# Strassen's seven products for the first feed-forward matrix, its result kept in DRAM

## The chip, the cores and the metric

One core of a Trainium2 chip runs the whole program. The metric is the device time of one execution in microseconds (us), as the median of several runs; one more execution, taken by the hardware profiler, gives the trace. Engines are named as in the profile: PE is TensorE's matrix multiplication and PEld its weight loading, DVE is VectorE, ACT is ScalarE, POOL is GpSimd, SP is SyncE, which here only issues DMAs.

## What is computed

One layer of a decoder for 1024 prompt tokens and 8 sample tokens, in fp32. Width D is 1024, the hidden width of the feed-forward part 2816, in 22 blocks of 128.

```
mod = silu(c) @ w_ada + b_ada            -> shift1, scale1, gate1, shift2, scale2, gate2
h   = x * (1 + scale1) + shift1
[q,k,v | rq,rk,rv,rg | ga,gb] = h @ w_in
A   = dilated window attention(q,k,v) @ w_att_out
B   = (silu(rg) * groupnorm(retention(rq,rk,rv))) @ w_ret_out
x   = LN1(alpha * x + gate1 * ((sigmoid(ga) * A + sigmoid(gb) * B) @ w_o))
f_gate, f_up = split((x * (1 + scale2) + shift2) @ w_ffn_in)
x   = LN2(alpha * x + gate2 * ((silu(f_gate) * f_up) @ w_ffn_out))
```

The outputs are both x, the prompt's caches and state, and the sample caches moved on by one row (rolled).

## The kernel before

Activations lie transposed in SBUF, features on the 128 partitions and tokens along the columns. An fp32 product is made of three products of rounded parts: `mm3` (L186 to L193) does hi x hi, hi x lo and lo x hi for each block k of 128 input features, and accumulates in PSUM. Weights come in by `wload`/`wcols` (L172 to L184): an SP-queue DMA of 512 KB into a raw buffer, a ScalarE cast to hi (L154), a subtraction for lo (L155) on VectorE, or on POOL for `w_o`. Raw, hi and lo have three buffers each; other tiles live in equal slots that are handed out and taken back in program order. PSUM banks are `dbank` (three), `abank` and `bbank` (two each), `obank` (one). A list scheduler orders each engine's instructions by modelled readiness, and each engine and queue then works in that order.

`dense` (L195 to L201) runs one weight block over the token chunks and calls the evacuation of each. The modulation for the later gates (`ada_rest`, L227 to L238) is 8 groups of 512 columns in four sub-steps of two k each; `dense` calls one sub-step after each chunk (`between`), in the gate stages at L844 and L855. The retention projection at L874 adds into the mix, stored as hi and lo (L866 to L872).

The `w_o` stage (L922 to L970) goes over the token chunks of TLAST, widths 392, 384 and 256 in this order, the first with the sample tokens: eight output blocks with `w_o` loaded anew for each chunk, then for every 128 tokens transposes back to token rows, layer norm, a store of the normalised rows to the DRAM tensor `xr`, transposes again, modulation and the split into `h2` hi and lo.

The feed-forward loop (L1029 to L1056) goes over portions of 6, 6, 6 and 4 hidden blocks. For each block f, gate and up weights are loaded, and for each token chunk come 24 matmuls for the gate, 24 for up, SiLU on ScalarE (L1041), the product on VectorE (L1044) and the split of `ff`. After a portion the second matrix goes over the portion's k, and `add_out` (L976) adds the gated result into `acc` in SBUF. The last portion's second matrix is resident (`load_resident`, L1016) and is run chunk by chunk (L1087) with the transposes (L1109), the residual, and `finish` (L1062), the second layer norm and store. `residual` (L1003) prepares alpha x from `xr` into `xo` during the loop.

The cache rolls are DMAs from DRAM to DRAM, on POOL's queue, one for each weight load while `rolling` is on (`roll`, L162): 78 entries, 24 of them empty spacers, 16 copies of 2 MB.

## Time and profile before

| | us |
|---|---|
| time, median of 3 runs | 1929.05 (1927.33 to 1930.64) |
| profiled execution, its own time | 1928.9 |
| its span in the trace | 1927.1 |
| PE busy | 1879.8 (98%) |
| DVE, ACT, POOL busy | 793.9, 551.3, 233.1 |
| mean granted clock of TensorE, share of full | 0.994 |

The trace's times count from the start of the span. A row of a timeline has start, duration, engine, line, operation, output and inputs, and in brackets the idle time before it and what ended that. A matmul's duration reaches into the next one, so the pitch is read from start to start.

### The profile page before, as it was taken

What the parts mean: (1) busy time and instruction counts of PE and PEld (TensorE: products, weight loads), DVE (VectorE), ACT (ScalarE), POOL (GpSimd) and SP (SyncE); (2) the same over time, 40 slices, a digit from 0 to 9 for tenths busy, and PEclk for the clock granted to TensorE, in tenths of its full rate; (3) what the DMA queues carried; (4) which work ended last, traced back from release to release, by engine and by line L of the source; (5) the groups of instructions that cost most, each with busy time, mean ns of one, the idle gap of its engine ahead of it and who ended that gap; (6) DMA issues with size and microseconds to landing.
All of it is one profiled execution on the core that took longest, in us unless ns stands there. A gap on an engine that the chain in (4) does not pass through costs nothing.

```text
span 1927.1 us, 29754 instructions
## 1 busy us (share of the span) xinstructions
PE 1879.8 (98%) x12406; PEld 1770.6 (92%) x12406; DVE 793.9 (41%) x1824; ACT 551.3 (29%) x1118; POOL 233.1 (12%) x313
## 2 busy tenths in 40 slices
PE   7999999999999999999999999999999999999996
PEld 5879889889899988889999999999999999999996
DVE  4733636676434431221453673221133332332337
ACT  3252332443434341121322553122222111211212
POOL 2000010320100000000003551000010000000015
PEclk9999999999999999999999999999999999999998
DMA  9312131681322343351123562223253643334332
GB/s 275 101 37 95 35 104 33 162 277 52 102 57 67 94 137 107 115 164 53 55 66 101 164 201 85 85 66 126 77 186 131 208 139 124 132 132 142 110 111 88
DMA packets 211016, 221.41 MB, mean 115 GB/s; under 512 B 7765, under 2 KB 186301, under 8 KB 210114
## 3 DMA queue, kind: packets, MB, share of 16 engines
q1 hardware_dynamic: 192338, 119.60, 21.7%
q0 software_dynamic: 18416, 99.82, 14.7%
q8 instruction: 97, 1.59, 0.3%
q14 instruction: 37, 0.30, 0.1%
q10 hardware_dynamic: 128, 0.10, 0.0%
HBM read 195.98 MB, written 67.54 MB: 137 GB/s over the span
## 4 chain that ended last, share of the span: by engine, by line
PE 88%; DVE 4%; DMA 3%; ACT 2%; issue 2%; SPq 1%; POOL 1%; DVEq 0%; POOLq 0%; ACTq 0%
PE ps_d L191 24%; PE ps_d L192 23%; PE ps_d L193 23%; PE ps_d L359 2%; PE ps_d L357 2%; PE ps_d L358 2%; DMA w_raw<-w_in 2%; PE ps_a L224 2%; PE ps_a L473 2%; PE ps_b L491 1%; PE ps_o L500 1%; DMA vb<-dv 1%; PE ps_o L745 1%; PE ps_a L747 1%; DVE h_lo L155 1%
## 5 line engine op out<-in xcount | busy, mean ns | idle before, releaser
L191 PE MATMUL ps_d<-h_hi,w_hi 128*128 128x384 f32 (+3 forms) x2064 | 664.4, 322 | 0.6 <-ACT tm L1041 0.6
L192 PE MATMUL ps_d<-h_lo,w_hi 128*128 128x384 f32 (+3 forms) x2064 | 662.0, 321 | 0.0
L193 PE MATMUL ps_d<-h_hi,w_lo 128*128 128x384 f32 (+3 forms) x2064 | 661.0, 320 | 0.0
L191 PEld LDWEIGHTS ps_d<-h_hi,w_hi 128*128 128x128 f32 x2064 | 388.2, 188 | 22.9 <-issue 17.3
L193 PEld LDWEIGHTS ps_d<-h_hi,w_lo 128*128 128x128 f32 x2064 | 388.2, 188 | 1.7 <-issue 1.2
L192 PEld LDWEIGHTS ps_d<-h_lo,w_hi 128*128 128x128 f32 x2064 | 388.0, 188 | 0.8 <-issue 0.4
L154 ACT CAST w_hi<-w_raw 128x1024 fp32r<-128x1024 f32 (+2 forms) x164 | 161.7, 987 | 479.1 <-PE ps_d L192 410.9
L155 DVE TENSOR_TENSOR w_lo<-w_raw,w_hi 128x1024 fp32r<-128x1024 f32 (+2 forms) x140 | 158.4, 1131 | 324.9 <-ACT w_hi L154 324.3
L1044 DVE TENSOR_TENSOR tm<-tm,ps_d 128x392 f32<-128x392 f32 (+2 forms) x66 | 33.8, 513 | 272.9 <-PE ps_d L193 271.4
L192 PE MATMUL ps_d<-ff_lo,w_hi 128*128 128x384 f32 (+1 forms) x432 | 138.2, 320 | 0.0
L191 PE MATMUL ps_d<-ff_hi,w_hi 128*128 128x384 f32 (+1 forms) x432 | 138.1, 320 | 0.0
L193 PE MATMUL ps_d<-ff_hi,w_lo 128*128 128x384 f32 (+1 forms) x432 | 138.1, 320 | 0.0
L359 PE MATMUL ps_d<-w_lo,h_hi 128*128 128x256 f32 x448 | 127.0, 284 | 0.7 <-DVE w_lo L155 0.7
L357 PE MATMUL ps_d<-w_hi,h_hi 128*128 128x256 f32 x448 | 127.4, 285 | 0.0
L358 PE MATMUL ps_d<-w_hi,h_lo 128*128 128x256 f32 x448 | 126.2, 282 | 0.0
L168 POOL COPY tick<-tk 1x1 f32<-1x1 f32 x54 | 11.2, 207 | 704.1 <-DVE tk L167 704.1
L357 PEld LDWEIGHTS ps_d<-w_hi,h_hi 128*128 128x128 f32 x448 | 84.3, 188 | 3.6 <-issue 3.1
L359 PEld LDWEIGHTS ps_d<-w_lo,h_hi 128*128 128x128 f32 x448 | 84.3, 188 | 2.7 <-issue 1.9
L154 ACT CAST ff_hi<-tm 128x392 fp32r<-128x392 f32 (+2 forms) x66 | 31.5, 477 | 188.4 <-DVE tm L1044 188.4
L358 PEld LDWEIGHTS ps_d<-w_hi,h_lo 128*128 128x128 f32 x448 | 84.4, 188 | 0.9 <-issue 0.7
L191 PEld LDWEIGHTS ps_d<-ff_hi,w_hi 128*128 128x128 f32 x432 | 81.3, 188 | 0.0
L192 PEld LDWEIGHTS ps_d<-ff_lo,w_hi 128*128 128x128 f32 x432 | 81.2, 188 | 0.0
(325 smaller groups left out, 2725.4 us busy)
## 6 DMA issues: line engine op xcount, KB each, us to landing
w_raw<-w_in SPq DMA_DIRECT2D x56, 512.0 KB, 4.1
w_raw<-w_ffn_in SPq DMA_DIRECT2D x44, 512.0 KB, 3.9
ada_raw<-w_ada SPq DMA_DIRECT2D x32, 512.0 KB, 4.6
sample_k<-cache_k POOLq DMA_DIRECT2D x8, 2047.0 KB, 10.2
sample_v<-cache_v POOLq DMA_DIRECT2D x8, 2047.0 KB, 10.0
w_raw<-w_o SPq DMA_DIRECT2D x24, 512.0 KB, 4.6
w_raw<-w_ffn_out SPq DMA_DIRECT2D x24, 384.0 KB, 4.4
ada_raw<-w_ada SPq DMA_DIRECT2D x32, 256.0 KB, 5.4
```

What stands on the lines that cost most here:

```text
L154: nc.scalar.copy(hi, raw)
L155: eng.tensor_sub(lo, raw, hi.bitcast(F32))
L191: nc.tensor.matmul(ps, whi[:, k0 + k, :], xhi[:, t0:t0 + n], start=f, stop=False)
L192: nc.tensor.matmul(ps, whi[:, k0 + k, :], xlo[:, t0:t0 + n], start=False, stop=False)
L193: nc.tensor.matmul(ps, wlo[:, k0 + k, :], xhi[:, t0:t0 + n], start=False, stop=l)
L224: nc.tensor.matmul(ps[32 * g:32 * g + 32], cs[:, k0 + k, :], w[:, k], start=k0 + k < 4, stop=k0 + k >= 4)
L357: nc.tensor.matmul(ps[:, j, :], xh, whi, start=k == 0, stop=False)
L358: nc.tensor.matmul(ps[:, j, :], xl, whi, start=False, stop=False)
L359: nc.tensor.matmul(ps[:, j, :], xh, wlo, start=False, stop=k == 7)
L473: nc.tensor.matmul(sb[hh][:, p, :nk], qT[p][r, 128 * bi:128 * bi + 128], kT[p][r, k0:k0 + nk], start=True, stop=True)
L491: nc.tensor.transpose(pb[:, j, :], pm[h][:, 128 * b:128 * b + 128], ident[:])
L1044: nc.vector.tensor_mul(tm[:, :n], tm[:, :n], pu)
```

## The change

The first feed-forward matrix is computed by Strassen's scheme (seven block products in place of eight). A 2 x 2 block product is taken over two halves of the input features, gate and up columns, and two token blocks of each 512-token half. For each half seven combinations X of the normalised input are made once (`combine`: four subtractions and seven splits for each 256-token chunk). For each hidden block, `pair_load` loads the gate and up weights (512 KB each) and makes the sums on POOL, `pair_split` splits them into hi and lo, and `pair_half` runs seven products of 12 matmuls with 260 (half 1) or 256 columns (half 0), adds the products up, and does SiLU and the product with up. The result of each block goes to the DRAM tensor `ffd`. The jobs run half 1 alone for the first three hidden blocks, both halves for the next 19, and half 0 for the first three at the end.

The second matrix then runs for half 1 and for half 0: the 22 blocks are read back and split (`xk`), the sum over all 22 k stays in PSUM, `w_ffn_out` is loaded for each half. `acc`, `xo` and the resident weights are gone; the residual is prepared on POOL when y is loaded. `w_o` and the retention projection go over chunks of 256, 256, 256 and 264 columns, `w_o` from the last chunk to the first. The later modulation is 16 steps of 256 columns over all k, one after each `dense` of the stages at L844 and L845.

```diff
-PORTIONS = (6, 6, 6, 4)
-TLAST = ((640, 392), (0, 384), (384, 256))
+QCH = ((0, 256), (256, 256), (512, 256), (768, 264))
+HALF = (256, 260)
+LEAD = 3
...
     def ada_rest():
-        for cg in range(4, 12):
-            ps = abank((128, 512))
-            for k0 in range(0, 8, 2):
-                raw = slots.alloc((128, 2, 512), name="ada_raw")
...
+        for cg in range(8, 24):
+            ps = abank((128, 256))
+            raws = [slots.alloc((128, 4, 256), name="ada_raw") for _ in range(2)]
...
-        dense(wcols(a["w_att_out"], 128 * f, nk=2), oa, mul)
+        dense(wcols(a["w_att_out"], 128 * f, nk=2), oa, mul, between=ada)
...
-        dense(wcols(w_in, C_GB + 128 * f), hT, sig, between=ada if f < 4 else None)
+        dense(wcols(w_in, C_GB + 128 * f), hT, sig)
...
-        dense(wcols(a["w_ret_out"], 128 * f), gs, evac)
+        dense(wcols(a["w_ret_out"], 128 * f), gs, evac, chunks=QCH)
...
+    def combine(X, c, x11, x21, x12, x22):
+        def put(p, v):
+            split(v, X[p][0][:, :, c], X[p][1][:, :, c])
+        put(1, x11)
+        put(2, x21)
+        put(3, x22)
+        nc.vector.tensor_sub(x11, x12, x11)
+        nc.vector.tensor_sub(x12, x22, x12)
+        nc.vector.tensor_sub(x22, x22, x11)
+        nc.vector.tensor_sub(x21, x21, x22)
+        put(6, x22)
+        put(5, x11)
+        put(7, x12)
+        put(4, x21)
...
+    def pair_load(i):
+        g, u, s_ = [stream.tile([128, 8, 128], F32, tag="raw", name="w_raw") for _ in range(3)]
+        for t, c0 in ((g, 128 * i), (u, D_FF + 128 * i)):
+            dma_w.dma_start(t[:], w_fi[:, c0:c0 + 128].rearrange("(k p) c -> p k c", p=128))
+        nc.gpsimd.tensor_add(s_[:, 4:8, :], u[:, 0:4, :], u[:, 4:8, :])
+        nc.gpsimd.tensor_sub(s_[:, 0:4, :], s_[:, 4:8, :], g[:, 0:4, :])
+        nc.gpsimd.tensor_sub(u[:, 0:4, :], g[:, 0:4, :], u[:, 0:4, :])
...
+    def pair_split(i, j):
...
+        if j < 3:
+            split((g, s_, u)[j][:], hi[:], lo[:])
+        else:
+            nc.gpsimd.tensor_sub(g[:, 4:8, :], g[:, 4:8, :], s_[:, 0:4, :])
+            split(g[:, 4:8, :], hi[:, 0:4, :], lo[:, 0:4, :])
+        if rolling[0]:
+            roll(hi)
...
+    def pair_half(i, half, after):
+        n, x = HALF[half], X[half]
+        t = slots.alloc((128, 4, 260), name="c4")
+        s1, u2, u3, c22 = [t[:, j, :n] for j in range(4)]
+        pa = obank((128, n))
+        product(pa, i, 0, 0, x[1], n, True)
+        nc.scalar.copy(s1, pa)
+        pg = dbank((128, n))
+        product(pg, i, 0, 1, x[2], n, True)
+        nc.vector.tensor_add(s1, s1, pg)
+        after(0)
+        product(pa, i, 1, 0, x[6], n, False)
+        nc.scalar.copy(u2, pa)
+        pd = dbank((128, n))
+        product(pd, i, 1, 1, x[5], n, True)
+        after(1)
+        product(pa, i, 2, 0, x[7], n, False)
+        nc.scalar.copy(u3, pa)
+        nc.vector.tensor_add(c22, u3, pd)
+        pf = dbank((128, n))
+        product(pf, i, 2, 1, x[4], n, True)
+        after(2)
+        nc.vector.tensor_add(u3, u3, pf)
+        product(pd, i, 3, 0, x[3], n, False)
+        after(3)
+        nc.vector.tensor_add(u2, u2, pd)
+        ff = slots.alloc((128, 2, 260), name="ff")
+        for j, (g, u) in enumerate(((s1, u3), (u2, c22))):
+            nc.scalar.activation(g, g, AF.Silu)
+            nc.vector.tensor_mul(ff[:, j, :n], g, u)
...
+        dma_o.dma_start(ffd[i, half].rearrange("p (a b) -> p a b", a=2)[:, :, :n], ff[:, :, :n])
...
+    for ci in (3, 2, 1, 0):
+        t0, n = QCH[ci]
...
+        if ci % 2 == 0:
+            X[ci // 2] = new_x()
+            combine_chunk(ci + 1)
+            combine_chunk(ci)
+
+    jobs = [(i, (1,)) for i in range(LEAD)] + [(i, (1, 0)) for i in range(LEAD, FFC)] + [(i, (0,)) for i in range(LEAD)]
+    rolling[0] = True
+    for q, (i, halves) in enumerate(jobs):
+        nxt = jobs[q + 1][0] if q + 1 < len(jobs) else None
...
+        if nxt is not None:
+            pair_load(nxt)
+            pair_split(nxt, 0)
+        for half in halves:
+            def after(j):
+                if half != halves[-1]:
+                    return
+                pair_drop(i, j)
+                if nxt is not None and j < 3:
+                    pair_split(nxt, j + 1)
+            pair_half(i, half, after)
...
+    for half in (1, 0):
+        n = HALF[half]
+        order = list(range(LEAD, FFC)) + list(range(LEAD))
+        xk = {}
+        for k in order:
+            raw = slots.alloc((128, 2, 260), name="ffr")
+            nc.sync.dma_start(raw[:, :, :n], ffd[k, half].rearrange("p (a b) -> p a b", a=2)[:, :, :n])
+            xk[k] = slots.alloc((128, 2, 2, 260), F32R, name="xk")
+            split(raw[:, :, :n], xk[k][:, 0, :, :n], xk[k][:, 1, :, :n])
...
+            for op, t in zip((OP.mult, OP.add), ln1):
+                nc.gpsimd.tensor_tensor(y[:rows], y[:rows], t[:rows], op=op)
...
+        for f in range(8):
+            pss = [dbank((128, n)) for _ in range(2)]
...
+            for k0, nk in ((0, 8), (8, 8), (16, 6)):
+                whi, wlo = wcols(w_fo, 128 * f, nk=nk, k0=k0)
+                for j, ps in enumerate(pss):
+                    for kk in range(nk):
+                        k = k0 + kk
+                        nc.tensor.matmul(ps, whi[:, kk, :], xk[k][:, 0, j, :n], start=k == 0, stop=False)
+                        nc.tensor.matmul(ps, whi[:, kk, :], xk[k][:, 1, j, :n], start=False, stop=False)
+                        nc.tensor.matmul(ps, wlo[:, kk, :], xk[k][:, 0, j, :n], start=False, stop=k == FFC - 1)
```

## Rows read from the trace of the kernel before

**Rows 1.** The page, part 1: busy us, share of the span, instructions.
```profile
PE 1879.8 (98%) x12406; PEld 1770.6 (92%) x12406; DVE 793.9 (41%) x1824; ACT 551.3 (29%) x1118; POOL 233.1 (12%) x313
```
**Rows 2.** Windows, feed-forward loop: window, length, PE, PEld, DVE, ACT, POOL, clock, DMA, GB/s.
```profile
1165.00:1864.00 699.00, 698.40 (x4440) 698.08 (x4439) 200.55 (x354) 138.81 (x227) 41.22 (x105) 1.00 0.36 123
```
**Rows 3.** Timeline of PE: first matmuls of runs with 256, 264, 384 columns.
```profile
1238.35 0.28 PE L191 MATMUL ps_d<-h_hi,w_hi 128*128 128x256 f32 x1
...
1244.02 0.34 PE L191 MATMUL ps_d<-h_hi,w_hi 128*128 128x392 f32 x1
...
1304.16 0.29 PE L191 MATMUL ps_d<-ff_hi,w_hi 128*128 128x264 f32 x1
...
1306.35 0.34 PE L191 MATMUL ps_d<-ff_hi,w_hi 128*128 128x384 f32 x1
...
1312.66 0.29 PE L191 MATMUL ps_d<-ff_hi,w_hi 128*128 128x264 f32 x1
```
**Rows 4.** Timeline of PE: first matmuls of w_o, FFN block, second matrix, next, last stage.
```profile
1037.66 0.45 PE L191 MATMUL ps_d<-m_hi,w_hi 128*128 128x392 f32 x1
...
1176.06 0.34 PE L191 MATMUL ps_d<-h_hi,w_hi 128*128 128x392 f32 x1
...
1289.33 0.34 PE L191 MATMUL ps_d<-ff_hi,w_hi 128*128 128x384 f32 x1
...
1357.39 0.34 PE L191 MATMUL ps_d<-h_hi,w_hi 128*128 128x392 f32 x1
...
1856.05 0.34 PE L191 MATMUL ps_d<-ff_hi,wr_hi 128*128 128x392 f32 x1
...
1915.98 0.45 PE L1109 MATMUL ps_a<-ident,acc 128*128 128x128 f32 x1 [2.09 <-DVE acc L984]
```
**Rows 5.** The chain that ended last: modulation of both shapes, and eight transposes.
```profile
33.54 1.00 PE ps_b L224 x16
...
706.86 0.98 PE ps_a L224 x4
...
1156.18 0.89 PE ps_b L952 x8
```
**Rows 6.** Groups by form: count, busy us, mean ns, idle before and its releasers.
```profile
L154 ACT CAST w_hi<-w_raw 128x1024 fp32r<-128x1024 f32 x132 | 138.4, 1050 | 357.1 <-PE ps_d L192 288.9 <-POOL w_lo L155 27.5 <-PE ps_d L358 26.4
L155 DVE TENSOR_TENSOR w_lo<-w_raw,w_hi 128x1024 fp32r<-128x1024 f32 x108 | 132.0, 1222 | 229.3 <-ACT w_hi L154 228.8
L155 POOL TENSOR_TENSOR w_lo<-w_raw,w_hi 128x1024 fp32r<-128x1024 f32 x24 | 57.9, 2414 | 47.6 <-ACT w_hi L154 47.5
...
L155 DVE TENSOR_TENSOR w_lo<-w_raw,w_hi 128x768 fp32r<-128x768 f32 x24 | 23.0, 958 | 44.1 <-ACT w_hi L154 43.9
```
**Rows 7.** Timeline of POOL, then of DVE, at the end of a w_o chunk.
```profile
1136.69 0.58 POOL L947 DMA_DIRECT2D xr<-x  x1 [2.87 <-DVE x L911]
1137.29 4.75 POOL L155 TENSOR_TENSOR w_lo<-w_raw,w_hi 128x1024 fp32r<-128x1024 f32 x2
1142.30 2.57 POOL L155 TENSOR_TENSOR w_lo<-w_raw,w_hi 128x1024 fp32r<-128x1024 f32 x1 [0.26 <-ACT w_hi L154]
...
1138.42 7.41 DVE L155 TENSOR_TENSOR h_lo<-tm,h_hi 128x128 fp32r<-128x128 f32 x8
```
**Rows 8.** Landings: weights, 1165 to 1860; then a cache copy issued at 1584.2.
```profile
DMA to landing us min/median/max: 3.3/3.9/9.3
...
DMA to landing us min/median/max: 10.0/10.0/10.0
```
**Rows 9.** The chain, then a window as in rows 2, around a late weight load.
```profile
367.10 27.07 DMA w_raw<-w_in
...
394.00:402.00 8.00, 5.90 (x24) 5.41 (x24) 5.35 (x9) 2.73 (x6) 0.10 (x1) 0.60 1.05 358
```
**Rows 10.** Timeline of DVE, tail: first and last of 14 operations for two blocks.
```profile
1916.89 0.75 DVE L1110 TENSOR_TENSOR y<-y,ps_a 128x256 f32<-128x256 f32 x2 [0.67 <-PE ps_a L1109]
...
1921.03 2.73 DVE L1081 SCALAR_TENSOR_TENSOR y<-y,bnr,ln_b 128x512 f32<-128x512 f32 x4
```

More of the change, by code (lines that the diff above doesn't have):

```diff
@@ L199, in dense @@
             evac(t0, n, ps)
-            if between:
-                next(between, None)
+        if between:
+            next(between, None)
     w_ada, w_in = a["w_ada"], a["w_in"]
@@ L912, in layer_norm @@
                                 op0=OP.subtract, op1=OP.mult)
[L914 to L916 removed]
     xr = dram.tile([T, D], F32, name="xr")
[L919 removed]
+    ffd = dram.tile([FFC, 2, 128, 520], F32, name="ffd")
+    w_fi, w_fo = a["w_ffn_in"], a["w_ffn_out"]
     rolling[0] = False
[L921 removed]
@@ new lines, in combine, with new_x @@
+    def combine(X, c, x11, x21, x12, x22):
[12 more added lines that the diff above has]
+        put(4, x21)
+    def new_x():
+        return {p: [slots.alloc((128, 4, 260), F32R, name=f"X{p}") for _ in range(2)] for p in range(1, 8)}
@@ new lines, in free_x, with combine_chunk @@
+    def free_x(X):
+        for t in X.values():
+            slots.free(*t)
+    h2s = late.tile([128, 8, NB], F32, name="h2s")
+    H2 = {}
+    X = [None, None]
+    def combine_chunk(ci):
+        p = slice(128 * (ci % 2), 128 * (ci % 2) + 128)
+        e, d = H2.pop(2 * ci), H2.pop(2 * ci + 1)
+        combine(X[ci // 2], p, e[:, 0:4, :], e[:, 4:8, :], d[:, 0:4, :], d[:, 4:8, :])
+        slots.free(e, d)
+        if ci == 3:
+            combine(X[1], slice(256, 260), h2s[:, 0:4, 0:4], h2s[:, 4:8, 0:4], h2s[:, 0:4, 4:8], h2s[:, 4:8, 4:8])
@@ new lines, in pair_drop, with product @@
+    def pair_drop(i, j):
+        for t in ring.pop((i, j)):
+            if any(t is e for e in extra):
+                extra[:] = [e for e in extra if e is not t]
+                slots.free(t)
+    def product(ps, i, j, part, xs, n, first):
+        (whi, wlo), (xhi, xlo) = ring[i, j], xs
+        for k in range(4):
+            w = 4 * part + k
+            nc.tensor.matmul(ps, whi[:, w, :], xhi[:, k, :n], start=first and k == 0, stop=False,
+                             skip_group_check=True)
+            nc.tensor.matmul(ps, whi[:, w, :], xlo[:, k, :n], start=False, stop=False, skip_group_check=True)
+            nc.tensor.matmul(ps, wlo[:, w, :], xhi[:, k, :n], start=False, stop=k == 3, skip_group_check=True)
@@ L991, in bcast @@
+    free_x(X[0])
+    rolling[0] = False
+    assert not copies, len(copies)
+    def bcast(names, scale=None):
         ts = []
@@ L1016, in load_resident @@
-    def load_resident(f0, np_):
-        for fp in range(4):
-            raw = stream.tile([128, np_, 256], F32, tag="raw", name="w_raw")
-            dma_w.dma_start(raw[:], w_fo[128 * f0:128 * (f0 + np_), 256 * fp:256 * fp + 256]
-                            .rearrange("(k p) c -> p k c", p=128))
-            hi = slots.alloc((128, np_, 256), F32R, name="wr_hi")
-            lo = slots.alloc((128, np_, 256), F32R, name="wr_lo")
-            split(raw[:], hi[:], lo[:])
-            wres.append((hi, lo))
@@ L1057, in tile_hybrid_decoder_step @@
-    assert not copies
-    f0 -= np_
-    for hi, lo in h2:
-        slots.free(hi, lo)
+    ln1 = bcast(("ln1_g", "ln1_b"), ALPHA)
     ln2 = bcast(("ln2_g", "ln2_b"))
```

272 lines of the change are left out of this document (122 added, 150 removed).

## Prediction

> **What bounds the kernel now.** I read the page's busy line first: TensorE is busy 98% of the span [rows 1]. The stretch of the feed-forward loop comes next: in its 699 us TensorE works 698.4 at full granted clock, while VectorE, ScalarE and POOL are busy 200.6, 138.8 and 41.2 [rows 2]. So each matmul saved there is time saved, until something else becomes late. Then I read the pitch of the matmuls, start to start: 48 of 256 columns from 1238.35 to 1244.02 are 118.1 ns each, 18 of 264 columns 121.7, 36 of 384 columns 175.3 [rows 3]. The pitch grows by 0.447 ns per column with next to nothing fixed, so narrower matmuls lose nothing; 260 columns lie between at 119.9, 392 at 178.9. Stage starts follow [rows 4]: w_o at 1037.66, the FFN period 22.65 us (three from 1176.06 to 1244.02), a second-matrix portion 68.06, the last stage 59.9, and 11.1 of tail to the span's end at 1927.1.
>
> **The change part by part, TensorE first.** All is set against the profiled execution's own 1928.9 us, which is 0.15 below the median of 1929.05.
> First matrix: a block of 128 hidden columns now takes 7 products of 12 matmuls for each token half, 84 x (119.9 + 118.1) ns = 19.99 us where it took 22.65 [rows 3, 4], 7/8 of the columns. Times 22: **-58.5**.
> Modulation: 32 sub-steps of 0.98 us, four 512-column matmuls each, become 16 steps with sixteen 256-column matmuls, of which such a step at 33.54 took 1.00 [rows 5]: 31.4 to 16, **-15.4**. Its transposes stay 32. Its loads, two of 512 KB for each step on SP's queue, land during the dense blocks between (11.3 and 2.8 us of matmuls by turns) and wait for room, not for data; if that cover were gone, up to 16 landings of about 4 us would show.
> w_o: 192 matmuls for each chunk width. Before, 192 x (178.9 + 175.3 + 118.1) ns = 90.7, and 9 token blocks x 16 transposes at 0.11 [rows 5] = 15.8: 106.5 without a stall. The stage took 1176.06 - 22.65 - 1037.66 = 115.75 [rows 4], so 9.2 are lost. After: 192 x (3 x 118.1 + 121.7) ns = 91.4, with transposes 107.2: **-8.5** before stalls, which I add below. The retention projection changes to the same four chunks: **+0.7**.
> Second matrix and last stage: 3 x 68.06 + 59.9 = 264.1 before [rows 4]. After: 8 x 22 x 3 matmuls on two banks and two halves, 1056 x (119.9 + 118.1) ns = 251.3, and 72 transposes at 0.11 = 7.9: 259.2, **-4.9**. The sums over portions, now in PSUM, were VectorE's and hidden.
> Tail: the last half has four token blocks to normalise after the last matmul instead of two. The two took VectorE from 1916.89 to 1923.76 [rows 10]; two more cost **+6.9**.
> Together **-79.8**, without any stall.
>
> **What becomes late.** Four places; the trace of before has none of them, so each is bounded from two sides.
> (1) **w_o and the first jobs, VectorE and POOL.** The 32 low-part splits of w_o are POOL's, 2.41 us each [rows 6]; 24 of them, and the four half-size additions for each of the first four weight pairs (16 x 1.2 = 19), run while VectorE makes the seven input blocks: 77 us of POOL. VectorE has 11 operations of 512 elements for each 256-token chunk, 4 x 11 x 0.69 us = 30 (0.69 by the slope between its 1024 and 768 forms, 1.03 ns per element [rows 6]), and some 24 for weight splits and SiLU products of these jobs. What happens when both run is in [rows 7]: eight VectorE splits of 128 elements, which that slope prices at 0.30 each, took 7.41 while three POOL splits ran, 5.0 too long. They ran in turn, not together. In turn the booking is 77 + 54 = 131 us, in a stretch of 122 us of matmuls (three chunks and four half-jobs): 9 short. POOL also waits in order at a store of the normalised block for VectorE (2.87 us, [rows 7]), with w_o's splits queued behind, and PE behind those: about 4 at each of three chunk ends, 12. I take 20. Lower end 9.2, what the stage loses now; upper end 1.67 us for each of 27 POOL operations, 45.
> The Trainium skill, "SBUF — State Buffer", section "Who interferes with whom", says that VectorE with two SBUF inputs and GpSimd reads lock each other out, and that the first to start holds the ports for its whole instruction. The trace agrees that one blocks the other; but there VectorE stayed out through two POOL splits on end (4.75 us) and got in at the 0.26 us gap [rows 7], where that rule would have let it in between them. By the rule (2) would be 0; by the row it is the upper end.
> (2) **Each job of the loop.** The next pair's three POOL additions (3.6 us) can hold a VectorE weight split, and behind it in VectorE's queue stands the addition that frees the bank for the last product. TensorE has two products (24 matmuls, 2.8 us) in hand: 0 if VectorE waits for one addition, 0.8 if for three. Over 19 jobs 0 to 15; I take 7. The store of a result on POOL's queue waits for the SiLU product, with the next additions behind it; they aren't needed for some 10 us, so nothing.
> (3) **The three trailing half-jobs** have 84 x 118.1 ns = 9.9 us of matmuls, and the next pair costs 3.9 landing [rows 8] + 3.6 on POOL + 1.05 + 1.22 for a split [rows 6] = 9.8, with nothing to spare: 4 (0 to 8).
> (4) **Going through DRAM.** Between the matrices most blocks of the first half are long in DRAM: 2, or 1 at the least. Between the halves the last three blocks of the second half (k = 0, 1, 2, which its first matmuls need) find room only when the first half's blocks are released. They stand on SP's queue, with the weight loads of the second half behind them. Two rounds of reload, each issue 0.4, landing 3.9 [rows 8] and a split of about 1.2, make 11; 8 if the first round is early, 15 if the granted clock falls as it did after the 27.07 us wait, to 0.60 between its two levels of 1.2 and 2.4 GHz for 8 us, 3.2 lost [rows 9].
> Reading 44 blocks back and loading the second matrix twice adds some 23 MB on queues that carry 123 GB/s there [rows 2]; hidden, as long as it is spread over 260 us. The products with PSUM inputs, the copies (ScalarE, some 8 of 20 us) and the residual on POOL have room beside 20 us of matmuls.
> Stalls: 20 + 7 + 4 + 2 + 11 = 44. **1928.9 - 79.8 + 44 = 1893.**
> A rule that speaks against narrow matmuls: the Trainium skill, "TensorE: Matmul & The Clock Gate", section "Back-to-back issue gap", gives a sustained 81 ns at 128 and 131 ns at 512 columns, by which 256 would cost about 98 and 384 about 114 (an estimate). Seven products would then take 16.5 us where six wide passes take 15.7, and the loop would be 5% slower. The rows have 118.1 and 175.3 in proportion to the columns, and 22.65 for the period, so it doesn't hold here.
>
> **The rivals.**
> A, **slower: weight loads behind the cache copies.** The copies from DRAM to DRAM are paced by weight splits: now four a job of 20 us, where before two fell in 22.65. With the spacers among them that is 16 copies of 2 MB in ten jobs, and one copy took 10.0 us to land, a load issued under it 9.3 instead of 3.9 [rows 8]. A pair has only three raw buffers, so no load starts before the pair ahead is split; its cast then stands in ScalarE's queue ahead of the copies that empty the single bank pa, and TensorE has only a few us in hand. If half of the 16 copies meet a load, 8 x 5.4 = 43: **1936**. Against it: such late loads are in the trace of before, and there TensorE lost 0.6 in 699 [rows 2]; loads come at the start of a job of 20 us, which covers one. It decides from eight meetings on (seven leave it within no change). Chance 0.22.
> B, **ports all the way:** (1) at 45 and (2) at 15: 1893 + 33 = **1926**, no change. For it [rows 7]; against it, only a part of VectorE's work there has two SBUF inputs. 0.10.
> C, **DRAM in one piece:** reading a block back waits for all writes to the scratch tensor. Then 19 earlier blocks come before k = 0: landing of the last write and of a read, 3.9 each [rows 8], and 20 blocks at 0.67 us (0.27 MB at the 400 GB/s of the 2 MB copy, read and written in 10.0), 21 instead of 2: **1912**. 0.08.
> D, **the narrow stream runs slower** than its pitch now, weight reads and four more banks' turns: 5% over the old period, 523 us instead of 440: 1893 + 83 = **1976**. Against it: 48 such matmuls in a row [rows 3]. 0.03.
> The forecast has 0.57.
>
> **How the numbers follow.** The likeliest is 1893, with 18 us of stalls at the least 1867. Upward the range takes in C, B and most of A: 1867 to 1940 leaves out D, the far end of A and some of the forecast's own tails, together under 2 in 10. Below and above by 0.2% is about what a measurement of this kernel can tell, 1925.2 to 1932.9 being no change. Faster: 0.57 + 0.08 (C) + 0.03 (B) + 0.03 (A with fewer meetings) = 0.71. Same: 0.05 (B) + 0.03 (A) = 0.08. Slower: 0.16 (A) + 0.02 (B) + 0.03 (D) = 0.21.
>
> **What would show it.** In the profile after: the start-to-start time of a two-half job, 20.0 to 20.8 us where I am right, with isolated ones near 25 for A; its matmul pitch 118 to 120 ns; modulation groups of 16 matmuls near 1.0 us; the w_o stage, first w_o matmul to first product, 107 plus about 15; a gap of about 11 between the two halves of the second matrix, and about 18 from the last transposes to the end. I am wrong if the page shows TensorE's idle time in the loop waiting on a weight load (A), on VectorE behind POOL in w_o (B), or on a read of the scratch tensor (C), and if the pitch is other than now (D).

## The result: 2023.3 us, 4.9% slower than before

The changed kernel takes 2023.32 us (2021.4 to 2027.1, 4 runs) against 1928.23 in the same session; the ratio is 1.0493, with a 95% interval of 1.0473 to 1.0514. Its profiled execution has a span of 2025.3 us, 98.2 longer than before. The forecast was 1893, in a range that ended at 1940.

First the windows view of the profile after, cut at the starts of the stages: window, length, busy us of PE, PEld, DVE, ACT and POOL with instructions, granted clock, DMA share, GB/s. The stretches are: `w_o` to the first product; three half-jobs ahead; nineteen jobs with both halves, with the last of them reaching into the next row; the trailing half-jobs; the second matrix for half 1 and for half 0; the tail.

```profile
1016.78:1144.69 127.91, 112.92 (x888) 109.01 (x888) 85.83 (x134) 65.61 (x121) 87.79 (x47) 0.95 0.57 177
1144.69:1199.56 54.87, 42.85 (x278) 40.41 (x279) 39.91 (x74) 26.01 (x48) 21.93 (x30) 0.83 0.43 147
1199.56:1649.36 449.80, 401.70 (x3111) 391.76 (x3110) 191.66 (x330) 139.06 (x263) 160.12 (x180) 0.95 0.45 155
1649.36:1710.78 61.42, 48.16 (x337) 47.14 (x336) 35.59 (x51) 26.96 (x49) 22.83 (x17) 0.85 0.63 199
1710.78:1862.19 151.41, 136.14 (x1097) 133.89 (x1097) 75.55 (x98) 44.05 (x64) 46.91 (x23) 0.95 0.47 142
1862.19:2007.60 145.41, 133.62 (x1082) 132.49 (x1081) 47.90 (x74) 37.42 (x51) 33.23 (x13) 0.94 0.29 87
2007.60:2025.30 17.70, 1.53 (x10) 0.79 (x8) 13.74 (x28) 1.44 (x5) 0.00 (x0) 0.67 0.31 119
```

Where the loop of before worked 698.4 of 699 us at full granted clock [rows 2], here TensorE is idle for a tenth of the loop, and no other engine is near full: VectorE 43%, ScalarE 31%, POOL 36%. So nothing is overloaded; things come late. The waits of PE in the nineteen jobs, up to 1649.4 (engine, line, releaser: us in total, times, longest):

```profile
PE ps_o L1034 <- ACT w_hi L158: 31.3, 14, 4.2
PE ps_d L1034 <- DVE c L1057: 7.6, 7, 1.5
PE ps_o L1034 <- ACT c L1051: 5.0, 3, 2.1
```

The casts of the next pair's weights lead (31.3 us in 14 jobs). One of these jobs, in the timelines of ACT, PE, SP's queue and POOL (start, duration, engine, line, operation; in brackets the idle time before and its end):

```profile
1526.77 0.38 ACT L1045 COPY c<-ps_o 128x260 f32<-128x260 f32 x1 [0.63 <-PE ps_o L1037]
1528.68 0.42 ACT L1067 ACTIVATE c<-c 128x260 f32<-128x260 f32 x1 [1.53 <-DVE c L1048]
1529.00 2.49 ACT L158 CAST w_hi<-w_raw 128x1024 fp32r<-128x1024 f32 x3
...
1530.08 0.39 PE L1034 MATMUL ps_o<-X,w_hi 128*128 128x260 f32 x1 [1.97 <-ACT w_hi L158]
...
1506.93 1.51 SPq L998 DMA_DIRECT2D w_raw<-w_ffn_in  x2
...
1508.64 0.52 POOL L174 DMA_DIRECT2D sample_v<-cache_v  x1
1518.56 1.28 POOL L999 TENSOR_TENSOR w_raw<-w_raw 128x512 f32<-128x512 f32 x1 [9.40 <-DMA w_raw<-w_ffn_in]
...
1520.46 1.30 POOL L1000 TENSOR_TENSOR w_raw<-w_raw 128x512 f32<-128x512 f32 x1
1521.72 1.29 POOL L1001 TENSOR_TENSOR w_raw<-w_raw 128x512 f32<-128x512 f32 x1
```

Read it backwards from PE. The product at 1530.08 waited for a cast. ScalarE began that cast at 1529.00, at once behind the SiLU of the new job's first two products (added up), and that SiLU waited for VectorE, which waited for the new job's first two products. The cast's data were ready at 1521.8, when POOL had ended L1000, so for 7 us the cast could have run and stood in line. Further back, POOL's addition had waited 9.4 us for a weight load, issued at 1507 to 1508.4, with a 2 MB copy issued at 1508.6 beside it. Landings of the first matrix's weights, from 1225 to 1550, min, median and max:

```profile
DMA to landing us min/median/max: 3.6/9.6/17.1
```

Before, the median was 3.9 [rows 8]. In the first fourteen jobs the three casts stand behind that SiLU, and in twelve of them the gap behind the second product is 2.25 or 2.26 us: a chain of the same instructions in a fixed order (copy, addition, SiLU, cast), not a matter of traffic. Nine of these twelve gaps also cost clock: it was 0.68 to 0.75 on average over the 5.3 us behind them, and 1.00 behind the other three. One gap, the 5.3 us behind it, and the rest of that job in the windows view:

```profile
1303.40:1305.60 2.20, 0.24 (x3) 0.03 (x1) 0.43 (x2) 1.39 (x3) 0.00 (x0) 1.00 0.34 119
1305.60:1310.90 5.30, 5.08 (x25) 4.75 (x26) 3.00 (x4) 1.86 (x4) 1.04 (x2) 0.68 0.50 145
1310.90:1325.00 14.10, 14.10 (x121) 14.10 (x120) 5.29 (x10) 3.33 (x7) 5.29 (x5) 1.00 0.49 189
```

The granted clock is 0.68 on average behind the gap, part of it at the lower level of 1.2 GHz, and 1.00 in the 14 us without a gap. In the loop up to 1649.4, spacings above 0.30 us between matmuls hold 59 us of lost time, and spacings between 0.17 and 0.30, about twice the usual 0.12 and so matmuls at the lower level, 20 us more.

The stages in us, from the starts of their first matmuls. The ideal is the sum of the prediction without a stall. The last three columns are experiments, told below; the half-jobs there are three ahead and three behind in E6 and E9, one and one in E13, with 21 full jobs.

| stretch | ideal | before | after | E6 | E9 | E13 |
|---|---|---|---|---|---|---|
| up to the retention projection | | 947.1 | 924.2 | 924.1 | 925.1 | 923.9 |
| retention projection | 91.3 | 90.6 | 92.6 | 92.6 | 92.6 | 92.4 |
| w_o to first product | 107.2 | 115.8 | 127.9 | 126.3 | 132.5 | 127.7 |
| half-jobs ahead | 30.2 (10.1) | | 54.9 | 55.9 | 51.6 | 20.4 |
| two-half jobs | 380 (420) | | 466.4 | 417.3 | 386.0 | 425.7 |
| trailing half-jobs | 29.8 (9.9) | | 44.8 | 43.2 | 40.7 | 17.3 |
| second matrix, half 1 | 131.0 | | 151.4 | 154.4 | 159.7 | 154.9 |
| second matrix, half 0 | 128.2 | | 145.3 | 134.2 | 132.8 | 132.5 |
| tail | 18.0 | 11.1 | 17.8 | 28.5 | 17.7 | 17.9 |

The two-half jobs are counted to the end of the last one's second half, at 1666.0. The stretch before the retention projection differs by some 5 us between executions of equal code there (924.0 to 929.4), so single runs are compared from the retention projection on as well.

### The profile page after: what moved, and what is told of

Read it like the earlier page. It is cut to its first block, busy times and chain, and to the rows that moved or that the text cites. A ratio compares the mean times of both kernels' runs of the same rounds, so it can differ in the third digit from the quotient of the medians.

```text
span 2025.3 us, 33789 instructions
## 1 busy us (share of the span) xinstructions
PE 1871.6 (92%) x13974; PEld 1766.6 (87%) x13974; DVE 960.3 (47%) x1993; ACT 678.5 (33%) x1327; POOL 467.9 (23%) x464
## 5 line engine op out<-in xcount | busy, mean ns | idle before, releaser
L195 PE MATMUL ps_d<-h_hi,w_hi 128*128 128x384 f32 (+1 forms) x1008 | 326.3, 324 | 0.0
L197 PE MATMUL ps_d<-h_hi,w_lo 128*128 128x384 f32 (+1 forms) x1008 | 323.8, 321 | 0.0
L196 PE MATMUL ps_d<-h_lo,w_hi 128*128 128x384 f32 (+1 forms) x1008 | 323.8, 321 | 0.0
L1034 PE MATMUL ps_d<-X,w_hi 128*128 128x260 f32 (+1 forms) x704 | 209.1, 297 | 14.9 <-DVE c L1057 11.2
L1195 PE MATMUL ps_d<-xk,w_hi 128*128 128x260 f32 (+1 forms) x704 | 202.2, 287 | 8.0 <-DVE xk L159 8.0
L1034 PE MATMUL ps_o<-X,w_hi 128*128 128x260 f32 (+1 forms) x528 | 159.0, 301 | 50.7 <-ACT w_hi L158 33.9
L1037 PE MATMUL ps_d<-X,w_lo 128*128 128x260 f32 (+1 forms) x704 | 204.8, 291 | 0.0
L1036 PE MATMUL ps_d<-X,w_hi 128*128 128x260 f32 (+1 forms) x704 | 204.2, 290 | 0.0
L1194 PE MATMUL ps_d<-xk,w_hi 128*128 128x260 f32 (+1 forms) x704 | 202.7, 289 | 1.4 <-DVE zs L1202 1.4
L1196 PE MATMUL ps_d<-xk,w_lo 128*128 128x260 f32 (+1 forms) x704 | 201.8, 287 | 0.0
L195 PEld LDWEIGHTS ps_d<-h_hi,w_hi 128*128 128x128 f32 x1008 | 189.4, 188 | 5.2 <-DVE A L846 3.3
L1034 PEld LDWEIGHTS ps_d<-X,w_hi 128*128 128x128 f32 x704 | 140.5, 200 | 20.8 <-DVE c L1057 13.4
L1036 PE MATMUL ps_o<-X,w_hi 128*128 128x260 f32 (+1 forms) x528 | 156.5, 296 | 0.0
L1036 PEld LDWEIGHTS ps_d<-X,w_hi 128*128 128x128 f32 x704 | 139.4, 198 | 0.0
```

What stands on the lines that cost most here:

```text
L195: nc.tensor.matmul(ps, whi[:, k0 + k, :], xhi[:, t0:t0 + n], start=f, stop=False)
L196: nc.tensor.matmul(ps, whi[:, k0 + k, :], xlo[:, t0:t0 + n], start=False, stop=False)
L197: nc.tensor.matmul(ps, wlo[:, k0 + k, :], xhi[:, t0:t0 + n], start=False, stop=l)
L1034: nc.tensor.matmul(ps, whi[:, w, :], xhi[:, k, :n], start=first and k == 0, stop=False, skip_group_check=True)
L1036: nc.tensor.matmul(ps, whi[:, w, :], xlo[:, k, :n], start=False, stop=False, skip_group_check=True)
L1037: nc.tensor.matmul(ps, wlo[:, w, :], xhi[:, k, :n], start=False, stop=k == 3, skip_group_check=True)
```

## The experiments

Two theories stood first. **Copies:** the cache copies make weight loads land late, and make the planned order put the casts late. **Ports:** VectorE is held up by POOL, whatever the loads do.

E1 to E3 and E5 to E8 were executed once each, and four executions of the change lie up to 5.7 us apart, so a time alone shows little there below 6 us. The stages repeat better: the nineteen jobs took 466.3 and 464.3 us in E7 and E8, whose edits lie elsewhere (466.4 after), and the second matrix's first half 150.3, 150.8 and 149.7 in E1, E2 and E7 (151.4 after). With each edit the scheduler also plans anew, so a few us in a stage can come of another order.

**E1, no large copies.**
```diff
+                if L < 2048:
+                    copies.append(tuple(...))
+                else:
+                    copies.append(None)
```


> The changed kernel without the sixteen 2 MB cache copies (left out; everything else is as it is). In the changed kernel a two-half job of the loop takes 24.4 to 26.5 us while these copies run (to 1520) and 20.5 to 21 after them. Theory 1: the copies cause it, because the next pair's loads land about 10 us late, in fact and in the scheduler's plan, so that the casts of products 2 to 4 are planned behind the SiLU of the next job. Then all 19 jobs take 20.3 to 21.5 us, the gap of 2.25 us behind the second product is gone, and the time falls by 50 to 75 us, to 1950 to 1975. Rival: VectorE held up by POOL, with the additions or the stores on POOL's queue as they are: then jobs stay at 24 us or more and the time falls by under 20 us.


The sixteen copies of 2 MB are left out. Measured: 1990.5 us, 33 less (42 less from the retention projection on). The nineteen jobs take 430.1 us instead of 466.4. The first five stayed at 23.9 to 26.0 us (0.5 MB copies ran beside the first three); of the others, all but the last (27.0) take 20.1 to 23.8. Neither expectation was met in full: the copies count, but something else holds jobs above 20.

**E2, casts first.** No instruction is changed, only the order: one copy of ScalarE is bound to come behind two casts. In the plan VectorE's addition of the second product and a few of TensorE's matmuls in each job move with it.
```diff
-        nc.scalar.copy(s1, pa)
+        with tc.issue_after(casts[i, 2].ins):
+            nc.scalar.copy(s1, pa)
```


> The changed kernel with all its copies; only the order on ScalarE is changed: the copy that empties the first product of a job is issued after that job's casts for products 2 and 3 (weights 1 and 2), which before stood behind it and the SiLU. Theory 1a: the order alone makes the 2.25 us gap, the data of the casts being there 3 to 6 us before: then the gap goes in most jobs, they take 20.5 to 22.5 us while copies run, and the time falls by 30 to 60 us, to 1965 to 1995. Theory 1b: the loads land so late behind the copies that the casts can't run earlier: then jobs stay at 24 us or more, and the time falls by under 15 us or grows.


Measured: 1998.2 us, 25 less (30 from the retention projection on), the jobs 440.9 in sum, half of them at 21.8 to 22.5 while copies run, the other half at 23.3 to 26.4. So order alone is worth 25.5 us in the jobs, at unchanged traffic: the time fell by less than theory 1a expected, and by more than 1b. What is left is hardly a wait for the casts any more. The first waits of PE in these jobs:

```profile
PE ps_d L1037 <- DVE c L1061: 22.0, 14, 3.1
PE ps_o L1037 <- ACT c L1049: 5.7, 2, 4.6
```

The timelines of ScalarE and VectorE in one of the jobs:

```profile
1487.39 1.05 ACT L158 CAST w_hi<-w_raw 128x1024 fp32r<-128x1024 f32 x1 [1.72 <-DMA w_raw<-w_ffn_in]
...
1488.48 1.23 DVE L159 TENSOR_TENSOR w_lo<-w_raw,w_hi 128x1024 fp32r<-128x1024 f32 x1 [3.52 <-ACT w_hi L158]
...
1489.68 0.40 DVE L1061 TENSOR_TENSOR c<-c,ps_d 128x260 f32<-128x260 f32 x1
```

The last product of the half writes into a bank that the addition at L1061 must read first; that addition stands behind a weight split, which waits for a cast, which waits for a load that is late. This is the mechanism of rival A, with VectorE's queue in it as well as ScalarE's.

**E3, reloads later.**
```diff
-            nc.sync.dma_start(raw[:, :, :n], ffd[k, half]...)
+            with tc.issue_after(last_load[0].ins):
+                nc.sync.dma_start(raw[:, :, :n], ffd[k, half]...)
```


> The changed kernel, with the reloads of the scratch tensor issued on SP's queue only after the last weight load of the first matrix. In the changed kernel the three half-jobs at the end take 61.4 us (1649.4 to 1710.8) where their matmuls need 29.8, and between 1647 and 1659 SP's queue stands at a reload with the second weight load of a pair behind it. If that wait is the cause: 61 falls to 35 to 45 us, and the time by 12 to 25 us (some of it given back at the start of the second matrix, where the reloads come later). Rival: the chain of one pair itself (load, three additions on POOL, cast, subtraction, with one set of raw buffers) takes 15 to 20 us whatever the queue does: then the three stay at 50 us or more and the time changes by under 8 us.


The 61.4 us named there hold four half-jobs' matmuls, 39.7 us, and not three: the second half of the last full job is among them. Measured: 2018.4 us, 5 less (12 from the retention projection on). Those four half-jobs take 48.9 us, between the two expectations. The full jobs fell by 8.5 (6.9 of it in the last), the trailing ones by 5.9 to 38.8 (42.4 and 42.3 in E7 and E8), and the second matrix's first half rose by 4.8. SP's queue after, and then in this run:

```profile
1646.61 0.37 SPq L998 DMA_DIRECT2D w_raw<-w_ffn_in  x1
1647.09 12.64 SPq L1168 DMA_DIRECT2D ffr<-ffd  x2
1664.00 0.38 SPq L998 DMA_DIRECT2D w_raw<-w_ffn_in  x1
```
```profile
1646.18 11.25 SPq L999 DMA_DIRECT2D w_raw<-w_ffn_in  x2
```

After, the second load of a pair was issued 17 us behind the first, with waiting reloads for 12.6 us of it. Without the reloads it came 11 us behind all the same; that it waits there for room in the raw buffers is read from the code. So both are true: the queue cost some, and the chain of one pair (load, additions, cast, subtraction, next load) takes 13 to 15 us where a half-job has ten of matmuls: the trailing jobs take 12.9 each here, and each half-job ahead 12.6 to 15.5 in E9 to E11 below.

**E4, the modulation alone,** put into the kernel before (the hunks of `ada_rest`, `dense` and the two calls).


> The kernel before with one part of the change alone: modulation in 16 steps of 256 columns after each dense of two stages. By the sum of the prediction it is 15.4 us faster (32 x 0.98 to 16 x 1.00), so 1913 or a ratio of 0.992; in the changed kernel the stretch up to the retention projection is 18.0 us shorter than before, which would give 0.9907. Rival: the larger loads come late, or the steps' evacuation blocks the banks: within 0.3% of before.


Measured: 1907.15 us against 1928.19, ratio 0.9901 (0.9881 to 0.9922). The stretch between the retention and its projection is 18.4 us shorter (256.1 to 237.7), against 15.4 in the sum. The timeline of PE around one step, before and in this run, has the rest:

```profile
706.53 0.33 PE L193 MATMUL ps_d<-h_hi,w_lo 128*128 128x384 f32 x1
706.79 1.05 PE L224 MATMUL ps_a<-ada_raw,cs 128*32 128x512 f32 x4
707.77 0.44 PE L191 MATMUL ps_d<-h_hi,w_hi 128*128 128x384 f32 x1
708.05 0.34 PE L192 MATMUL ps_d<-h_lo,w_hi 128*128 128x384 f32 x1
```
```profile
713.28 0.28 PE L193 MATMUL ps_d<-h_hi,w_lo 128*128 128x264 f32 x1
713.49 1.07 PE L224 MATMUL ps_a<-ada_raw,cs 128*32 128x256 f32 x16
714.49 0.45 PE L191 MATMUL ps_d<-oa_hi,w_hi 128*128 128x384 f32 x1
714.77 0.34 PE L192 MATMUL ps_d<-oa_lo,w_hi 128*128 128x384 f32 x1
```

The step itself is 0.98 or 1.00, as counted. But the last matmul ahead of it takes 0.26 instead of 0.175, and the first behind it 0.28: about 0.19 us for going in and out, 32 times before and 16 times now: 3.0 us, which is the rest. Whether it is the format or something else of such a step that costs this was not tried apart.

**E5, a bank for each product.**
```diff
-        product(pa, i, 1, 0, x[6], n, False)
-        nc.scalar.copy(u2, pa)
+        p6 = abank((128, n))
+        product(p6, i, 1, 0, x[6], n, True)
+        nc.vector.tensor_add(u2, s1, p6)
...
+        nc.vector.tensor_add(u3, u2, p7)
+        nc.vector.tensor_add(u2, u2, pd)
```


> The changed kernel with one edit in the loop: each of the seven products has a PSUM bank of its own (the banks of the transposes stand idle there), where products 1, 3 and 5 shared one and 4 and 7 another, so that a product had to wait until ScalarE or VectorE had emptied the one before; two copies of ScalarE become additions of VectorE and one addition is new. In the changed kernel TensorE waits 29 us in the loop for these copies and additions, and each wait lowers the clock behind it. If the banks are a cause of their own: the time falls by 25 to 45 us, the jobs take 22 to 23.5 us while copies run. If only the planned order of the casts counts (as in the run with the casts first): the 2.25 us gap stays, jobs stay at 24 us or more, and the time falls by under 10 us.


Measured: 2001.6 us, 22 less (26 from the retention projection on); the jobs 438.0 in sum, 22.3 to 26.9 while copies run and 19.96 to 20.14 after them. What is left are the casts:

```profile
PE ps_a L1034 <- ACT w_hi L158: 22.2, 14, 2.7
PE ps_b L1034 <- ACT w_hi L158: 3.5, 14, 0.5
```

So the shared banks are a cause of their own, and with the copies gone by, a job has no stall at all. That the time fell by less than the jobs (28.4), and less than the 25 to 45 expected, is the second matrix's first half: it rose to 160.7, with no copies beside it; why is not shown.

**E6, copies elsewhere.** `rolling` is on from the gate stages to the retention projection and in the second matrix, off in the first; the large copies come first.


> The changed kernel with all 54 cache copies moved out of the first matrix: with their pacing and spacers as they are, the large ones first, they start in the gate stages and the retention projection (32 weight loads) and end in the second matrix (46 more). The run without the 2 MB copies still had the 0.5 MB ones in its first seven jobs, and those stayed at 24 to 26 us. If the copies of either size are the cause: all 19 two-half jobs take 20.2 to 21.5 us, 385 to 405 in sum for 450, and the time falls by 45 to 65 us, 0 to 15 given back where the copies now are. Rival: jobs 3 to 8 are slow because of the start (VectorE and POOL behind with the input blocks): then they stay at 24 us, and only the later ones fall.


Measured: 1978.4 us, 45 less (49 from the retention projection on); the jobs 417.3 in sum, not 385 to 405, the first of them 25.2, the next two 20.5 and 20.2, so not slow from the start as the rival had it. Now the shared bank alone holds them (`pa`, emptied by ScalarE at L1052 and L1046):

```profile
PE ps_o L1035 <- ACT c L1052: 18.2, 11, 2.3
PE ps_o L1035 <- ACT c L1046: 6.3, 5, 3.8
```

The tail grew to 28.5 us, with POOL's last normalisations (1951.1 to 1962.8) beside VectorE's.

**E7, w_o's low parts on VectorE.**
```diff
-            mm3(ps, wcols(a["w_o"], 128 * f, eng=nc.gpsimd), ...)
+            mm3(ps, wcols(a["w_o"], 128 * f), ...)
```


> The changed kernel with the low parts of w_o made by VectorE instead of POOL. In the changed kernel the stretch from the first w_o matmul to the first product takes 127.9 us (107.2 without a stall), and the first three half-jobs 54.9 instead of 30. If VectorE and POOL locking each other out is what costs there: 10 to 20 us less in that stretch. If VectorE has too much to do by itself (32 x 1.22 = 39 us more): equal or slower, by up to 20 us. The three half-jobs come out of the weight chain by either theory and stay within 5 us.


Measured: 2022.1 us; from w_o to the first product 120.6 instead of 127.9, less than the 10 to 20 of the first theory. With the same edit in E10 that stretch takes 132.6, without it in E13 127.7. So POOL's part in the loss at w_o isn't shown: the edit moved the stretch by 7 us down in one order and by 5 up in the other.

**E8, the residual on VectorE.**
```diff
-                nc.gpsimd.tensor_tensor(y[:rows], y[:rows], t[:rows], op=op)
+                nc.vector.tensor_tensor(y[:rows], y[:rows], t[:rows], op=op)
```


> The changed kernel with the residual's product and sum (18 operations of 1024 elements when y is loaded) on VectorE instead of POOL. Between the two halves of the second matrix VectorE's splits of the reloaded blocks take 2.8 us instead of 0.7, one behind each POOL operation, and TensorE waits 8.6 us for the transposed rows' addition queued behind them. If the lock-out is the cause: that gap falls under 3 us and the time by 6 to 12 us. Rival: the reloads themselves come late (room and landing), and the gap stays at 7 us or more; the time within 4 us.


Measured: 2015.1 us, 8 less; the second matrix's first half 143.3 instead of 151.4. POOL, DVE and PE after, at the end of that half, and DVE in this run:

```profile
1853.52 2.79 POOL L1182 TENSOR_TENSOR y<-y,ln_g 128x1024 f32<-128x1024 f32 x1
1856.39 2.68 POOL L1182 TENSOR_TENSOR y<-y,ln_b 128x1024 f32<-128x1024 f32 x1
...
1854.10 5.52 DVE L159 TENSOR_TENSOR xk<-ffr,xk 128x512 fp32r<-128x512 f32 x2
...
1860.01 0.90 PE L1215 MATMUL ps_a<-ident,z 128*128 128x128 f32 x3 [8.31 <-DVE y L1216]
```
```profile
1844.19 1.93 DVE L159 TENSOR_TENSOR xk<-ffr,xk 128x512 fp32r<-128x512 f32 x3
```

Two splits of 512 elements take 5.52 us while POOL works, three take 1.93 when it doesn't. TensorE's waits for the additions behind them (L1216) fell from 9.6 us in the second matrix, 8.3 in one gap, to 1.7, as expected. This is the mechanism of [rows 7] at a place where the prediction didn't look for it. One thing differs: the first of the two splits ended at 1856.86, so VectorE got in between two POOL operations 0.08 us apart, where in [rows 7] it stayed out through two that ran on end.

**E9, E3 and E5 to E8 together,** with one spacer for each large copy and two more queues cleared: the stores of the first half's blocks go to POOL's queue, since on SP's (1904.76 to 1910.8 after) four weight loads stood behind one that waited for POOL, and PE stood still from 1903.5 to 1909.9 (6.4 us, for ScalarE, which had waited 8.3 us for one of these loads); and those blocks are finished one for each output block.


> The whole change with the causes found so far taken away together: a bank for each product, the cache copies outside the first matrix (one spacer for each large copy instead of one and two), reloads issued after the last weight load, the residual and w_o's low parts on VectorE, the stores of the first half's blocks on POOL's queue instead of SP's (where weight loads stood behind one for 5 us), and those blocks finished one by one from the first output block on. If the causes add up: from the run with the copies elsewhere (1978), 20 less in the 19 two-half jobs (400 to 380, each 20.0), 12 in the trailing jobs, 6 at w_o, 15 to 25 in the second matrix, 5 to 10 in the tail: 1900 to 1925, so faster than before by 0 to 1.5%. Rival: the waits only change places (the queues of VectorE and SP take over): 1940 or more, and some two-half jobs stay above 21.5 us.


Measured: 1938.09 us against 1925.31, ratio 1.0064 (1.0043 to 1.0085). The jobs in the windows view:

```profile
1201.90:1587.90 386.00, 382.22 (x3195) 381.88 (x3194) 235.94 (x421) 115.92 (x193) 134.70 (x122) 0.99 0.28 86
```

Nineteen jobs in 386.0 us, the first 26.4 and the others 19.89 to 20.19: the loop's loss of 86 us is gone but for 6, all in the first job. POOL's additions of weights run in these jobs as before, so the theory of the ports has no part in them once the banks and the copies are out of the way. The second half of the second matrix is at 132.8 too. But w_o (132.5) and the first half of the second matrix (159.7) got worse by 5 and 8, so the rival is half right: in those two stretches the waits changed places.

**E10 and E11, fewer half-jobs ahead** (`LEAD` 1 and 2 in E9).


> The same with one half-job ahead instead of three (LEAD 1), so one at the end. A half-job has 10 us of matmuls, but a weight pair takes some 15 (one set of raw buffers: load, additions, cast, subtraction, then the next load), so each half-job loses 5 at both ends; two of each less save about 20: 1885 to 1905. Rival: the second half's input blocks, for which the half-jobs make time, aren't ready after one: TensorE waits 10 to 30 us there, and the time is equal or slower.

> The same with two half-jobs ahead (LEAD 2). Between the runs with three and with one: about 10 less than with three if the weight chain sets the half-jobs' time; if the input blocks of the second half set the end of the first jobs, no better than with three.


Measured: 1927.34 (ratio 1.0007, 0.9992 to 1.0021) and 1933.42 (1.0044, 1.0022 to 1.0067): 11 and 5 less than with three, half of what was expected. With one half-job ahead (E10), the half-jobs at both ends take 41.3 us instead of 92.4, 51 less, and the full jobs, two more of them, 422.8 instead of 386.0, 37 more.

**E12, copies from the retention stage on** (E10, with w_o's low parts on POOL again).


> The version with one half-job ahead (1927 us), with w_o's low parts on POOL again and the cache copies started with the retention's weight loads, so that 14 small ones are left for the second matrix. In that version the stretch from w_o to the first product took 132.6 us with VectorE making the low parts, 126 to 127.9 with POOL making them in the runs that had it so; the first half of the second matrix took 156 us (131 without a stall) with 22 copies beside it. If both are separate causes: w_o back to 126 to 128, the second matrix's first half to 140 to 150, the stretch up to the retention projection unchanged within 5 us: 1905 to 1920, faster than before. Rival: the copies now hold the loads of the retention stage, where TensorE already waits for loads: the retention projection starts 5 to 20 us later and the time stays at 1920 to 1935.


Measured: 1940.26 us, ratio 1.0070 (1.0048 to 1.0091). The rival was right: the retention projection starts at 942.8 instead of 927.6. w_o is back at 127.5. The second matrix's first half is at 153.0 instead of 156.0, with 13 small copies issued beside it instead of 23. Ten copies fewer took off 3 us; that it can be slow without any shows in E5 (160.7).

**E13, one half-job ahead, reloads as in the change** (E10 without the edits of E3 and E7).


> The version with one half-job ahead (1927 us), with w_o's low parts on POOL again and the reloads of the scratch tensor free to go ahead of the last weight loads; copies as in that version. In the runs that held the reloads back, the first half of the second matrix took 156 to 160 us, in those that didn't, 143 to 154 (131 without a stall). If the held-back reloads cost there, and VectorE at w_o: 126 to 128 us for w_o (132.6), 143 to 152 for that half (156), with one trailing half-job 2 to 5 us longer: 1908 to 1920, faster than before by 0.4 to 1%. Rival: the late half comes of the 22 reloads and their splits whenever they start, in few free slots: then it stays at 153 or more, and the time at 1919 to 1927.


Measured: 1918.62 us against 1924.36, ratio 0.9966 (0.9954 to 0.9979): a third of a per cent below before, and 5% below the changed kernel, with the whole change in it. The profiled execution, at 1914.6, lies at the lower end of its runs. The full jobs, and then the first half of the second matrix:

```profile
1164.40:1590.10 425.70, 421.49 (x3530) 421.07 (x3529) 267.59 (x480) 132.49 (x222) 145.61 (x129) 1.00 0.28 87
1607.44:1762.35 154.91, 139.08 (x1099) 134.80 (x1097) 77.23 (x150) 48.90 (x73) 22.27 (x53) 0.95 0.59 185
```

21 jobs in 425.7 us, clock 1.00. But the first half of the second matrix stays at 154.9, by the rival's number. There the waits are for reloaded blocks and for one weight cast (5.2 and 4.9 us), and the reloads of this run took 2.7 to 12.6 us to land, median 7.0. Whether fewer bytes, more free slots or another order would mend that wasn't tried.

Set against before by stretches, this run's profile is 34.9 us shorter from the first product to the second matrix (463.4 against 22 periods of 22.65), but 30.1 longer from the second matrix on and 12.0 longer at w_o. What makes it faster in sum is the stretch ahead of the retention projection, 23.2 shorter, most of it the modulation. And E4, the modulation alone, is faster still (1907.15, ratio 0.9901): in no version tried here did the rest of the change gain anything beside the modulation.

## Why the prediction was wrong

**Right, as working.** The matmul arithmetic held: 19.97 us for a job without a stall in E9 to E13, 19.99 predicted from the pitch in [rows 3]. So did the tail (17.8, predicted 18.0), and the modulation to within 3 us (E4). Rival D is out by the same 19.97. The retention projection took 2.0 more and not 0.7; why wasn't looked into.

**The step that failed** is the list of what becomes late: 44 us there, 184.3 measured (20.7 + 24.7 + 86.4 + 15.0 + 20.4 + 17.1, the stages' differences from the ideal). That difference of 140 is the whole error, but for small ones: 1927.1 - 79.8 + 184.3, with 2.6 more saved up to the retention projection by the modulation and 4.9 by a stretch that didn't change, 1.3 lost in the retention projection and 0.2 saved in the tail, makes the 2025.3 of the span to within 0.1.

- (2) *Each job of the loop*: 7, at the most 15; it was 86.4. Two mechanisms were in it, and the runs took them apart. Copies and their plan: -49.1 without them (E6). The shared banks: -28.4 with a bank for each product (E5). With both, -80.4 (E9). The two are nearly additive. E9 also holds the reloads back, but E13 doesn't, and its 21 jobs lose 6.3 in all. Of the first part, the planned order alone is 25.5 (E2). The prediction had looked at one place only, the addition behind a weight split, and had priced it by POOL. The addition does wait there (22.0 us in E2), but for a split that waits for a late load and its cast; POOL hardly held the splits of these jobs, which took 1.224 us at the median between 1225 and 1550, and 1.225 before. It had counted the copies of ScalarE as busy time ("some 8 of 20 us") and not as the thing that a single bank makes every second product wait for.
- (1) *w_o and the first jobs*: 20, at the most 45; it was 20.7 at w_o and 24.7 in the half-jobs, 45.4 together, more than twice the forecast. What it is made of is only partly shown. The half-jobs are held by the chain of one pair: each one more costs 12.6 to 15.5 us ahead (E9 to E11) for some 10 of matmuls, and that chain wasn't in the sum. At w_o, 13 to 27 remained in every order that was tried; of some 15 us of waits there, 4.9 are for POOL's low parts and 5.9 for ScalarE's evacuation, which the sum had not named. That 20.7 comes near the 20 of the sum is luck.
- (3) *The trailing half-jobs*: 4; it was 15.0. The sum had put 9.8 us of one pair beside 9.9 of matmuls as if the next pair's load ran beside this pair's split. With one set of raw buffers it can't: "no load starts before the pair ahead is split" stood in rival A, and wasn't used here. The chain is 13 to 15 (E3, E9 to E11), and at this end SP's queue came on top.
- (4) *Through DRAM*: 2 and 11; it was 20.4 and 17.1. The 11 was reckoned from reloads; the gap that stands between the halves, 8.3 us at the end of the first one's stretch, came of the residual (E8). Some 6 to 8 of the 20.4 are POOL locking VectorE out (E8), by a part of the change, the residual, that the prediction had put down as having room; what holds the rest stays open (E13). Of the 17.1, 6.4 is the store on SP's queue ahead of weight loads. It is 4.3 to 4.6 in E9 and E13, with these stores on POOL's queue; in E6, with the stores as they were, it is 6.0, with 10.7 more in the tail.

**Rival A** named the right thing and the wrong size. It had the late loads, the in-order queue and the single bank; it expected a few meetings of a load with a copy, 8 of 5.4 us. In fact they met in nearly every job (nine of the twelve pairs loaded from 1232 to 1507 have a load that took 8.8 to 17.1 us, and the last made POOL wait 9.4), since the split that triggers a copy is also what frees the raw buffers for the next loads: both are issued within 2 us (1506.93 and 1508.64 in the rows above). And the evidence against it, that before lost only 0.6 us with such loads about [rows 2, 8], was no evidence, because before the loads ran ahead of need: in that loop 65 casts waited 196.8 us for TensorE to free their buffers, and none of them for a load. About half of the cost of the copies was in the plan (25.5 of 49.1): with copies in it, the scheduler put three casts behind the next job's SiLU in fourteen jobs running.

**The form of the error**: A, B and the forecast were weighed as alternatives. They were parts of one kernel, and added up: A's 49, B's 45 at (1), though only in part for its reason, and the shared banks without any late load, which no rival had.

## What to carry to other kernels

When a change makes the steps between evacuations shorter, the slack that hid in-order queues shrinks with it; look in the changed code for each bank, buffer or queue of which there is one, and price the wait, not the busy time. Rivals that act at different places add up, and the range has to hold their sum. And where DMAs are paced by compute, look at what else the same event releases: two things that one event starts will meet each time. And try each part of a change alone: here one part by itself (E4) was faster than the whole in every version.

## What the runs showed of the hardware that was not expected

Going from the rounded format's matmuls to plain fp32 ones and back costs about 0.19 us, beside the matmuls themselves (0.26 and 0.28 us for neighbours that take 0.175 otherwise). A gap of 2.25 us lowered the granted clock to 0.68 to 0.75 on average over the next 5.3 us in nine of twelve cases and left it at 1.00 in three, and the gaps of the loop cost about a third as much again: 59 us in gaps, 20 in slow matmuls. VectorE got in between two POOL operations 0.08 us apart, one split for each (E8), where it had stayed out through two on end before [rows 7]. And a weight load of 512 KB landed in 9.6 us at the median beside paced copies, 4.2 where none ran (E9).
